# adaLN weights read by column halves, with a fixed order of loads, half sums over k for two units, and unread matmuls

## The chip, the core and the metric

The kernel is one program on one core of a Trainium2 chip. A core has a matrix engine (PE; the loads of its stationary operand are listed apart as PEld), a vector engine (DVE), a scalar engine (ACT), GpSimd (POOL), and SP, which here only issues DMAs. Each engine works through its own list of instructions in order and waits at semaphores for the others. The metric is the device time of one execution in microseconds (us), the median of several runs.

## The reference, cut to what matters

The layer is a diffusion-transformer block over 1024 latent tokens and 256 context tokens, width 1024. Only its beginning concerns this change: a conditioning vector gives a shift and a scale for each channel, the normalised tokens are scaled and shifted by them, and the result goes through one wide input projection.

```python
mod_lat = jax.nn.silu(c) @ w_ada[l] + b_ada[l]          # c: (1, 1024), w_ada: (1024, 6 * 1024)
mod_ctx = jax.nn.silu(c_ctx) @ w_ada[l] + b_ada[l]
sh1, sc1, gt1, sh2, sc2, gt2 = jnp.split(mod_lat[:, None, :], 6, axis=-1)
...
h_lat = modulate(rmsnorm(x_lat, norm_pre_mix[l]), sh1, sc1)   # h * (1 + scale) + shift
h_ctx = modulate(rmsnorm(x_ctx, norm_pre_mix[l]), csh1, csc1)
... = jnp.split(h_lat @ w_in, SPLITS, axis=-1)                # w_in: (1024, 4096)
```

Attention, a gated linear recurrence, the output projection and a 16-expert mixture follow; the change does not touch them.

## The kernel before, in words

Channel index d is cut into KT = 8 groups of 128, called k. The start stage does the following.

**The adaLN product** (lines 584 to 592). Of `w_ada` the first 2048 columns (shift, then scale) are needed here. A load (`load_ada`, line 500) brings one k and 1024 columns, 512 KB in pieces of 4 KB, into one of six buffers `aw`; sixteen loads bring all. Two matmuls per load add to one PSUM tile `mod_ps`, which the vector engine has cleared. After the sixteenth the tile is copied (lines 602, 603), transposed (607), and three DVE instructions make the columns `scc` and `shc` for all 8 values of k (618 to 620).

**The tokens.** They come as ten tiles of 128, in pairs p = 0 to 4 (pair 4 is the context). For each tile ACT squares and sums (`square_x`, 577), DVE and POOL make the reciprocal root (105, 106), DVE scales the tile (582). `trans_pair` transposes a pair on PE, 16 transposes into four PSUM tiles `tpx`, each for two values of k. `mod_pair` applies scale and shift: for k with k % 4 > 1 on ACT (646), else on DVE (648), then splits the result into a rounded high part on ACT (651) and the rest on DVE (652), four values of k in one instruction. The high and low parts `h_hi`, `h_lo` are what the projection reads.

**The projection.** A `Job` is a slice of columns of `w_in`; its weights are loaded (141) and split likewise into `whi` and `wlo` (150, 151). The first job has 256 columns, and `unit_N` makes one unit of it: two token tiles, 8 values of k, three matmuls for each (hi by hi, lo by hi, hi by lo: 185 to 187), 48 matmuls of 256 columns. Five units, one for each pair, make the first job; `ev_v` (258) copies a finished unit out, so this copy marks the end of a unit. The first unit is issued as two halves, one token tile each.

**What sets the order.** Within `manual_schedule` (line 521 to 670) PE, DVE and ACT run in the order of the code; SP is not in that set. Outside, a scheduler lays out each engine's list when the program is built. All loads spoken of are issued by SP: first the sixteen of `w_ada`, then the tokens' tiles 0 and 1, the first job's weights, the other tiles. The ring of `aw` buffers also holds the two context tiles.

Of the kernel before, what the change touches and what calls it, by code (L numbers as in the profile page):

```python
# [8 lines left out]
F32 = mybir.dt.float32  # L9
# [11 lines left out]
D = 1024  # L21
# [52 lines left out]
def layer(ctx: ExitStack, tc, a, out):  # L74
# [57 lines left out]
    class Job:  # L132
# [4 lines left out]
        def load(self):  # L137
            kk = 1024 // self.w
            for g in range(KT // kk):
# [4 lines left out]
        def split(self):  # L144
            kk = 512 // self.w
            for g in range(KT // kk):
# [25 lines left out]
    def unit_N(job, ppool, t, halves=False):  # L172

        pp = []

        def half(j):
            def f():
                if j == 0:
                    pp.append(ppool.tile([128, 512], F32, name="pp", bufs=2))
                o = pp[0][:, j * 256:(j + 1) * 256]  # L180
                c, z = divmod(t + j, 4)
                s = slice(z * 128, (z + 1) * 128)
                for k in range(KT):
                    whi, wlo = job.piece(job.hi, k), job.piece(job.lo, k)
                    nc.tensor.matmul(o, h_hi[c][:, k, s], whi, start=(k == 0), stop=False)  # L185
                    nc.tensor.matmul(o, h_lo[c][:, k, s], whi, start=False, stop=False)  # L186
                    nc.tensor.matmul(o, h_hi[c][:, k, s], wlo, start=False, stop=(k == KT - 1))
                if j == 1:
                    job.evac(pp[0], t)
            return f  # L190
        a, b = half(0), half(1)

        def both():
            a()
            b()
        return [a, b] if halves else both
# [297 lines left out]
    ps_p, ps_st = pool("start_ps", space=PSUM)  # L494
    mod_p, mod_st = pool("mod_ps", space=PSUM)
# [4 lines left out]
    def load_ada(i):  # L500
        aw = st_p.tile([128, 1024], F32, name="aw", bufs=6)
        nc.sync.dma_start(aw, adaw[:, i // 2, i % 2 * 1024:(i % 2 + 1) * 1024])
        aw_t.append(aw)

    def load_x(i):
# [7 lines left out]
        else:  # L513
            xts[i] = st_p.tile([128, D], F32, name="aw", bufs=6)
        nc.sync.dma_start(xts[i], a[src].rearrange("o (i p) d -> (o i) p d", p=128)[j])

    for k in range(6):
        load_ada(k)
# [8 lines left out]

    mod_ps = mod_p.tile([128, 512], F32, name="mod_ps")
    nc.vector.memset(mod_ps, 0.0)
# [20 lines left out]
    def small_vectors():  # L550
        nc.vector.tensor_copy(masks.rearrange("p l s -> p (l s)"), mf[:, :masks.shape[1] * 64])

        cols_ps = ps_p.tile([128, 512], F32, name="tp", bufs=2)
# [30 lines left out]
    for i in range(2 * KT):  # L584
        if i == 8:
            small_vectors()
        for n in range(2):
            q = 64 * (i % 2) + 32 * n
            nc.tensor.matmul(mod_ps[q:q + 2, :], silu[:, i // 2, :], aw_t[i][:, n * 512:(n + 1) * 512],
                             start=(i < 2), stop=(i // 2 == KT - 1))  # L590
        if i + 6 < 2 * KT:
            load_ada(i + 6)
    load_x(0)
    load_x(1)
    jobs[0].load()
    for i in range(2, 6):
        load_x(i)
    jobs[1].load()
    for i in range(6, 10):
        load_x(i)  # L600
    mods = st_p.tile([128, 512], F32, name="mods")
    nc.scalar.copy(mods[:, 0:256], mod_ps[:, 0:256])
    nc.vector.tensor_copy(mods[:, 256:512], mod_ps[:, 256:512])
    mod_st.close()
    modc_ps = ps_p.tile([128, 512], F32, name="tp", bufs=2)
    for j in range(4):
        nc.tensor.transpose(modc_ps[:, 128 * j:128 * j + 128], mods[:, j * 128:(j + 1) * 128], ident)
    shc = const.tile([128, KT, 2], F32, name="shc")
    scc = const.tile([128, KT, 2], F32, name="scc")

    mc = modc_ps.rearrange("p (j m n z) -> p m n j z", j=4, m=2, n=2)[:, :, :, :, 0:2]

    def four(ap):
        return ap.rearrange("p (n j) c -> p n j c", n=2)

    def both(i):
        return four(cols[:, i:i + 8, None].to_broadcast([128, 8, 2]))
    nc.vector.tensor_tensor(four(scc), mc[:, 1], both(34), op=OP.add)
    nc.vector.scalar_tensor_tensor(four(scc), four(scc), 1.0, both(0), op0=OP.add, op1=OP.mult)
    nc.vector.tensor_tensor(four(shc), mc[:, 0], both(26), op=OP.add)  # L620
    square_x(0)
    scale_x(0)
    square_x(1)
    scale_x(1)

    tp_p, tp_st = pool("tp_ps", space=PSUM)
    tps = {}

    def trans_pair(p):

        for g in range(4):
# [6 lines left out]
    def mod_pair(p):  # L638
# [3 lines left out]
        hf = [st_p.tile([128, 4, 256], F32, name="hf", bufs=2) for g in range(2)]  # L642
        for k in range(KT):
            tp, o = tps[p, k // 2][:, k % 2, :], hf[k // 4][:, k % 4, :]
            if k % 4 > 1:
                nc.scalar.activation(o, tp, AF.Identity, scale=scc[:, k, j:j + 1], bias=shc[:, k, j:j + 1])
            else:
# [1089 lines left out]
```

## Time and profile before

| | us |
|---|---|
| median of 3 runs | 1536.4 (1534.77 to 1536.62) |
| the profiled execution, own time | 1533.79 |
| its span in the profile | 1532.0 |
| first matmul of the first unit | 40.65 |
| copy of the fifth unit's result begins | 80.54 |

All times below are microseconds from the start of the span. In the timeline view each row has start, duration, engine, line, operation, output<-input, shape, count; in square brackets stands how long the engine had been idle and what released it. Consecutive equal instructions are merged in one row with their count. The line numbers of the kernel before and of the changed one differ: 185 to 187 become 189 to 191, 589 becomes 598, 636 becomes 628, 648 becomes 641, 652 becomes 645, 582 becomes 585, 502 becomes 506, 515 becomes 519.

### The profile page before, as it was taken

How to read it: one execution, taken by the hardware profiler on the slowest of the kernel's cores; microseconds unless marked ns; L12 is line 12 of the kernel's file. 1: busy time of each engine (PE TensorE's matmuls, PEld its weight loads, DVE VectorE, ACT ScalarE, POOL GpSimd, SP SyncE). 2: the span in 40 equal slices, each digit the busy share in tenths (PEclk: the TensorE clock that was granted, in tenths of full speed). 3: DMA queues.
4: the chain of work that ended last, by engine and by line, in shares of the span. 5: the costliest groups of instructions: out<-in, count | busy, mean ns of one | idle time of the engine just before them, and what ended most of it. 6: DMA issues, size and time to landing. Idle time of an engine off the chain costs nothing. (4 is left out here: it accounts for less than half of the span.)

```text
span 1532.0 us, 23371 instructions
## 1 busy us (share of the span) xinstructions
PE 1451.2 (95%) x8889; PEld 1193.5 (78%) x8889; DVE 1155.3 (75%) x1578; ACT 871.8 (57%) x1342; POOL 127.5 (8%) x139
## 2 busy tenths in 40 slices
PE   5999999999999997999999978999999999999993
PEld 1888998888977786999977845888888888888871
DVE  2727472859268668999936577999999999999984
ACT  2733442444211107988943324888888888888881
POOL 2100000000000001011001000111111111100013
PEclk9999999999999998999999999999999999999997
DMA  9210110100056617236026696999999999999966
GB/s 336 88 55 29 29 29 28 29 28 29 17 180 195 184 37 196 54 78 183 29 96 247 225 340 234 369 378 383 383 383 383 383 383 375 380 385 385 380 208 124
DMA packets 160332, 316.28 MB, mean 206 GB/s; under 512 B 13790, under 2 KB 50870, under 8 KB 160220
## 3 DMA queue, kind: packets, MB, share of 16 engines
q1 hardware_dynamic: 149616, 277.99, 50.4%
q0 software_dynamic: 9408, 33.54, 9.3%
q10 hardware_dynamic: 1196, 3.26, 0.6%
q8 instruction: 70, 1.15, 0.3%
q14 instruction: 42, 0.34, 0.1%
HBM read 274.36 MB, written 29.38 MB: 198 GB/s over the span
## 5 line engine op out<-in xcount | busy, mean ns | idle before, releaser
L1396 DVE TENSOR_TENSOR mlo<-mraw,mhi 128x1024 fp32r<-128x1024 f32 x332 | 398.2, 1223 | 19.1 <-ACT mhi L1395 15.0
L1395 ACT CAST mhi<-mraw 128x1024 fp32r<-128x1024 f32 x332 | 348.4, 1051 | 78.7 <-PE g L1546 28.8
L166 PE MATMUL pp<-h_hi,whi 128*128 128x512 f32 (+1 forms) x480 | 180.1, 375 | 0.0
L167 PE MATMUL pp<-h_lo,whi 128*128 128x512 f32 (+1 forms) x480 | 178.3, 371 | 0.0
L168 PE MATMUL pp<-h_hi,wlo 128*128 128x512 f32 (+1 forms) x480 | 178.0, 371 | 0.0
L150 ACT CAST whi<-wraw 128x512 fp32r<-128x512 f32 x64 | 39.6, 621 | 121.1 <-PE pp L167 59.1
L881 DVE TENSOR_REDUCE sm<-s 128x1 f32<-128x1280 f32 x64 | 95.3, 1491 | 13.1 <-PE s L876 10.7
L166 PEld LDWEIGHTS pp<-h_hi,whi 128*128 128x128 f32 x480 | 90.5, 188 | 17.6 <-ACT T L478 0.9
L168 PEld LDWEIGHTS pp<-h_hi,wlo 128*128 128x128 f32 x480 | 90.4, 188 | 17.1 <-issue 1.7
L1545 PE MATMUL g<-mhi,xhi 128*128 128x512 f32 x256 | 102.2, 399 | 0.5 <-ACT xhi L1525 0.5
L167 PEld LDWEIGHTS pp<-h_lo,whi 128*128 128x128 f32 x480 | 90.5, 189 | 15.6 <-issue 0.9
L1547 PE MATMUL g<-mlo,xhi 128*128 128x512 f32 x256 | 101.2, 395 | 0.2
L1546 PE MATMUL g<-mhi,xlo 128*128 128x512 f32 x256 | 101.1, 395 | 0.0
L1545 PE MATMUL u<-mhi,xhi 128*128 128x512 f32 x256 | 101.0, 394 | 0.0
L1547 PE MATMUL u<-mlo,xhi 128*128 128x512 f32 x256 | 100.9, 394 | 0.0
L1546 PE MATMUL u<-mhi,xlo 128*128 128x512 f32 x256 | 100.7, 393 | 0.0
L1650 PE MATMUL my<-mhi,hlo 128*128 128x512 f32 x240 | 97.7, 407 | 0.0
L1649 PE MATMUL my<-mhi,hhi 128*128 128x512 f32 x240 | 95.6, 398 | 0.0
L1651 PE MATMUL my<-mlo,hhi 128*128 128x512 f32 x240 | 95.2, 396 | 0.0
L185 PE MATMUL pp<-whi,h_hi 128*128 128x256 f32 x320 | 92.7, 290 | 2.0 <-ACT h_hi L651 2.0
L343 DVE TENSOR_TENSOR X<-X,T 128x640 f32<-128x640 f32 (+1 forms) x112 | 78.2, 761 | 20.4 <-ACT KM L321 12.8
L186 PE MATMUL pp<-whi,h_lo 128*128 128x256 f32 x320 | 91.8, 287 | 0.9 <-DVE h_lo L652 0.9
(331 smaller groups left out, 3149.5 us busy)
## 6 DMA issues: line engine op xcount, KB each, us to landing
mraw<-in_w_down_dram SPq DMA_DIRECT2D x128, 512.0 KB
mraw<-in_w_gate_dram SPq DMA_DIRECT2D x106, 512.0 KB
mraw<-in_w_up_dram SPq DMA_DIRECT2D x106, 512.0 KB
wraw<-in_w_in_dram SPq DMA_DIRECT2D x32, 512.0 KB
aw<-in_w_ada_dram SPq DMA_DIRECT2D x64, 256.0 KB
T<-in_w_gate_dram SPq DMA_DIRECT2D x22, 512.0 KB
T<-in_w_up_dram SPq DMA_DIRECT2D x22, 512.0 KB
aw<-in_w_ada_dram SPq DMA_DIRECT2D x16, 512.0 KB
```

What stands on the lines that cost most here:

```text
L166: nc.tensor.matmul(pp[:, :n], whi, hh, start=(k == 0), stop=False)
L167: nc.tensor.matmul(pp[:, :n], whi, hl, start=False, stop=False)
L168: nc.tensor.matmul(pp[:, :n], wlo, hh, start=False, stop=(k == KT - 1))
L881: nc.vector.tensor_reduce(self.sm[:, m:m + 1], s, axis=AX.X, op=OP.max, negate=True)
L1395: nc.scalar.copy(hi, r)
L1396: nc.vector.tensor_sub(lo, r, hi)
L1545: nc.tensor.matmul(o, x.hi[:, k, :], hi[:, kk, :], start=(k == 0), stop=False)
L1546: nc.tensor.matmul(o, x.lo[:, k, :], hi[:, kk, :], start=False, stop=False)
L1547: nc.tensor.matmul(o, x.hi[:, k, :], lo[:, kk, :], start=False, stop=(k == 7))
L1649: nc.tensor.matmul(y[:, ns], x.hh[:, k, :], hi[:, ns], start=(k == 0), stop=False)
L1650: nc.tensor.matmul(y[:, ns], x.hl[:, k, :], hi[:, ns], start=False, stop=False)
L1651: nc.tensor.matmul(y[:, ns], x.hh[:, k, :], lo[:, ns], start=False, stop=(k == 7))
```

## The change

1. `w_ada` is read by column halves: a load now brings one k and 2 x 512 columns (half of the shift columns and the same half of the scale columns, pieces of 2 KB). Eight loads make the first half (k groups 0 to 3 of `scc`, `shc`), eight more the second. Each half has its own clear, copy, transposes and three DVE instructions (`ada_out`). The ring has seven buffers, and the PSUM tile `tp` has one buffer in place of two.
2. SP joins the manual order: tokens 0 and 1, the eight loads of the first half, the first job's weights around tokens 2 and 3, the eight of the second half, then the rest.
3. `unit_N` takes `parts`: for the first two units part 0 sums k = 0 to 3 for both token tiles, part 1 the rest. A matmul of zeros opens the PSUM tile. `trans_pair` and `mod_pair` can do one half of the values of k.
4. `keep_on` issues matmuls whose result nobody reads: ten after the first `ada_out`, eight after the second.

The diff, cut:

```diff
-    def unit_N(job, ppool, t, halves=False):
+    def unit_N(job, ppool, t, parts=1):
...
+                    if parts > 1:
+                        nc.tensor.matmul(pp[0], zero1[:, 0:128], zero1, start=True, stop=False)
+                for j in range(2):
...
+                    for k in range(i * KT // parts, (i + 1) * KT // parts):
...
     def load_ada(i):
-        aw = st_p.tile([128, 1024], F32, name="aw", bufs=6)
-        nc.sync.dma_start(aw, adaw[:, i // 2, i % 2 * 1024:(i % 2 + 1) * 1024])
+
+        aw = st_p.tile([128, 2, 512], F32, name="aw", bufs=7)
+        src = adaw[:, i % KT, 0:2 * D].rearrange("p (m c) -> p m c", m=2)
+        nc.sync.dma_start(aw, src[:, :, i // KT * 512:(i // KT + 1) * 512])
...
-    ms = tc.manual_schedule(engines={nc.tensor.engine, nc.vector.engine, nc.scalar.engine})
+    ms = tc.manual_schedule(engines={nc.tensor.engine, nc.vector.engine, nc.scalar.engine, nc.sync.engine})
     ms.__enter__()
+    load_x(0)
+    load_x(1)
+    for k in range(KT - 1):
+        load_ada(k)
...
+    def ada_mm(i):
+
+        if i % KT == 0:
+            mod_ps.append(mod_p.tile([128, 512], F32, name="mod_ps"))
+            nc.vector.memset(mod_ps[-1], 0.0)
+        for m in range(2):
+            nc.tensor.matmul(mod_ps[-1][32 * m:32 * m + 2, :], silu[:, i % KT, :], aw_t[i][:, m, :],
+                             start=(i % KT == 0), stop=(i % KT == KT - 1))
...
+    u0, u1 = (unit_N(jobs[0], pps, t, parts=2) for t in (0, 2))
+    norm_pair(0)
+    for i in range(KT):
+        ada_mm(i)
+        if i == 0:
+            load_ada(KT - 1)
+            jobs[0].load(0)
+            load_x(2)
+            load_x(3)
+            jobs[0].load(1)
+        else:
+            load_ada(KT - 1 + i)
+        if i == 3:
+            small_vectors()
+            trans_pair(0)
+    load_ada(2 * KT - 1)
+    load_x(4)
+    load_x(5)
+    jobs[1].load()
+    for i in range(6, 10):
+        load_x(i)
+    ada_out(0)
+    jobs[0].split(0)
+    mod_pair(0, (0,))
+    keep_on(10)
+    u0[0]()
     norm_pair(1)
-    u0[0]()
-    trans_pair(1)
+    jobs[0].split(1)
+    ada_mm(8)
+    trans_pair(1, (0, 1))
+    ada_mm(9)
+    ada_mm(10)
+    mod_pair(1, (0,))
+    ada_mm(11)
+    ada_mm(12)
+    u1[0]()
+    for i in range(13, 16):
+        ada_mm(i)
+    ada_out(1)
+    keep_on(8)
+    mod_pair(0, (1,))
+    trans_pair(1, (2, 3))
+    mod_pair(1, (1,))
+    norm_pair(2)
     u0[1]()
+    trans_pair(2, (0, 1))
+    u1[1]()
+    trans_pair(2, (2, 3))
     ms.__exit__(None, None, None)
```

From the sixth unit on the lists of all engines hold the same rows in the same order as before. Three places where they differ follow.

SP's loads at the start, before (-) and now (+); `outT_hg` and `xpair` are the tokens' tiles, `aw` the adaLN weights, `wraw` the projection's:

```order
-L502 DMA aw<-in_w_ada_dram 128x1024 x16
-L515 DMA outT_hg_77<-in_x_dram 128x1024 x2
-L141 DMA wraw<-in_w_in_dram 128x4x256 x2
-L515 DMA outT_hg_78<-in_x_dram 128x1024 x2
-L515 DMA xpair<-in_x_dram 128x1024 x2
+L519 DMA outT_hg_77<-in_x_dram 128x1024 x2
+L506 DMA aw<-in_w_ada_dram 128x2x512 x8
+L141 DMA wraw<-in_w_in_dram 128x4x256
+L519 DMA outT_hg_78<-in_x_dram 128x1024 x2
+L141 DMA wraw<-in_w_in_dram 128x4x256
+L506 DMA aw<-in_w_ada_dram 128x2x512 x8
+L519 DMA xpair<-in_x_dram 128x1024 x2
```

The tokens 0 and 1 stand ahead of all weights now, and tokens 2 and 3 and the first job's weights ahead of the second half of `w_ada`.

The vector engine from the first shift and scale on, first before (`outT_hg_77` are tokens 0 and 1, `outT_hg_78` tokens 2 and 3):

```order
L620 TENSOR_TENSOR shc<-tp,cols 128x16
L105 TENSOR_SCALAR st<-st 128x1
L582 TENSOR_SCALAR outT_hg_77<-outT_hg_77,st 128x1024
L105 TENSOR_SCALAR st<-st 128x1
L582 TENSOR_SCALAR outT_hg_77<-outT_hg_77,st 128x1024
L151 TENSOR_TENSOR wlo<-wraw,whi 128x512 x4
L648 TENSOR_SCALAR hf<-tpx,scc,shc 128x256 x4
L652 TENSOR_TENSOR h_lo_85<-hf,h_hi_84 128x4x256 x2
```

and now:

```order
L617 TENSOR_TENSOR shc<-tp,cols 128x8
L151 TENSOR_TENSOR wlo<-wraw,whi 128x512 x2
L641 TENSOR_SCALAR hf<-tpx,scc,shc 128x256 x2
L645 TENSOR_TENSOR h_lo_85<-hf,h_hi_84 128x4x256
L105 TENSOR_SCALAR st<-st 128x1
L585 TENSOR_SCALAR outT_hg_78<-outT_hg_78,st 128x1024
L105 TENSOR_SCALAR st<-st 128x1
L585 TENSOR_SCALAR outT_hg_78<-outT_hg_78,st 128x1024
L151 TENSOR_TENSOR wlo<-wraw,whi 128x512 x2
L596 MEMSET mod_ps 128x512
L641 TENSOR_SCALAR hf<-tpx,scc,shc 128x256 x2
L645 TENSOR_TENSOR h_lo_85<-hf,h_hi_84 128x4x256
```

The clear of the second half's `mod_ps` stands behind the scaling of tokens 2 and 3 and the split of the second piece of weights; the ninth adaLN product on PE needs it.

PE around the transposes of tokens 4 and 5, which the changed program issues between part 1 of the first unit (`pp_299`) and part 1 of the second (`pp_374`):

```order
L190 MATMUL pp_299<-whi_341,h_lo0_85 128x256
L191 MATMUL pp_299<-wlo_342,h_hi0_84 128x256
L628 MATMUL tpx_490<-ident_67,xpair_250 128x128 x4
L628 MATMUL tpx_495<-ident_67,xpair_250 128x128 x4
L189 MATMUL pp_374<-whi_337,h_hi0_84 128x256
L190 MATMUL pp_374<-whi_337,h_lo0_85 128x256
```

Before, the transposes of tokens 4 and 5 (`xpair_225`) stood behind the whole first unit (`pp_328`) and ahead of the whole second one (`pp_494`):

```order
L186 MATMUL pp_328<-whi_298,h_lo0_85 128x256
L187 MATMUL pp_328<-wlo_299,h_hi0_84 128x256
L636 MATMUL tpx_428<-ident_67,xpair_225 128x128 x4
L636 MATMUL tpx_433<-ident_67,xpair_225 128x128 x4
L636 MATMUL tpx_438<-ident_67,xpair_225 128x128 x4
L636 MATMUL tpx_443<-ident_67,xpair_225 128x128 x4
L185 MATMUL pp_494<-whi_286,h_hi0_84 128x256
L186 MATMUL pp_494<-whi_286,h_lo0_85 128x256
```

In both programs the unit behind the transposes cannot begin until tokens 4 and 5 are scaled.

## Rows read from the trace of the kernel before

**Rows 1.** The page: span, busy time of each engine, GB/s in 40 equal slices.
```profile
span 1532.0 us, 23371 instructions
PE 1451.2 (95%) x8889; PEld 1193.5 (78%) x8889; DVE 1155.3 (75%) x1578; ACT 871.8 (57%) x1342; POOL 127.5 (8%) x139
GB/s 336 88 55 29 29 29 28 29 28 29 17 180 195 184 37 196 54 78 183 29 96 247 225 340 234 369 378 383 383 383 383 383 383 375 380 385 385 380 208 124
```

**Rows 2.** Windows: PE, PEld, DVE, ACT, POOL busy us; granted clock; DMA share; GB/s.
```profile
25.00:30.00 5.00, 3.99 (x18) 0.37 (x16) 0.00 (x0) 0.00 (x0) 0.00 (x0) 1.00 1.02 407
35.00:40.00 5.00, 3.33 (x15) 3.06 (x15) 4.44 (x9) 3.39 (x7) 0.00 (x0) 0.67 1.05 382
40.00:45.00 5.00, 3.47 (x15) 3.28 (x16) 3.24 (x5) 4.89 (x9) 0.94 (x2) 0.68 1.06 396
45.00:50.00 5.00, 5.00 (x45) 5.00 (x44) 3.80 (x9) 4.31 (x9) 1.26 (x3) 0.98 0.53 157
70.00:75.00 5.00, 5.00 (x44) 5.00 (x43) 0.62 (x1) 0.22 (x1) 0.00 (x0) 1.00 0.02 3
```

**Rows 3.** Timeline, 0 to 82 us: adaLN products, shift and scale, units one and five.
```profile
16.52 0.09 PEld L589 LDWEIGHTS mod_ps<-aw,silu 128*2 128x2 f32 x4 [1.21 <-DMA aw<-in_w_ada_dram]
21.64 0.09 PEld L589 LDWEIGHTS mod_ps<-aw,silu 128*2 128x2 f32 x4 [1.19 <-DMA aw<-in_w_ada_dram]
29.32 1.03 PE L589 MATMUL mod_ps<-aw,silu 128*2 128x512 f32 x4 [0.26 <-DMA aw<-in_w_ada_dram]
32.06 0.17 DVE L620 TENSOR_TENSOR shc<-tp,cols 128x16 f32<-128x16 f32 x1
40.65 0.38 PE L185 MATMUL pp<-whi,h_hi 128*128 128x256 f32 x1 [2.04 <-ACT h_hi L651]
74.78 0.65 ACT L258 COPY V<-pp 128x256 f32<-128x256 f32 x2 [5.06 <-PE pp L187]
80.54 0.65 ACT L258 COPY V<-pp 128x256 f32<-128x256 f32 x2 [0.22 <-PE pp L187]
```

**Rows 4.** Lines by form, 0 to 82 us: count, busy us, mean ns.
```profile
L652 DVE TENSOR_TENSOR h_lo<-hf,h_hi 128x1024 fp32r<-128x1024 f32 x10 | 11.8, 1221 | 1.7 <-ACT h_hi L651 1.7
L651 ACT CAST h_hi<-hf 128x1024 fp32r<-128x1024 f32 x10 | 10.1, 1059 | 0.4 <-DVE hf L648 0.4
L648 DVE TENSOR_SCALAR hf<-tpx,scc,shc 128x256 f32<-128x256 f32 x20 | 10.0, 538 | 0.0
L646 ACT ACTIVATE hf<-tpx,shc,scc 128x256 f32<-128x256 f32 x20 | 10.3, 568 | 2.8 <-PE tpx L636 2.3 <-DVE h_lo L652 0.4
L151 DVE TENSOR_TENSOR wlo<-wraw,whi 128x512 fp32r<-128x512 f32 x8 | 5.2, 687 | 8.3 <-ACT whi L150 8.3
```

**Rows 5.** Timeline: squares of tokens 2 and 3, scaling of token 3.
```profile
41.44 1.06 ACT L577 ACTIVATE sq<-outT_hg 128x1024 bf16<-128x1024 f32 x1
45.20 0.75 DVE L582 TENSOR_SCALAR outT_hg<-outT_hg,st 128x1024 f32<-128x1024 f32 x1 [0.66 <-POOL st L106]
```

**Rows 6.** Timeline, PE: 256-column matmuls at the low clock, transposes at either.
```profile
43.14 0.41 PE L185 MATMUL pp<-whi,h_hi 128*128 128x256 f32 x1
43.35 0.41 PE L186 MATMUL pp<-whi,h_lo 128*128 128x256 f32 x1
35.28 3.33 PE L636 MATMUL tpx<-ident,outT_hg 128*128 128x128 f32 x15 [1.10 <-DVE outT_hg L582]
50.80 1.91 PE L636 MATMUL tpx<-ident,xpair 128*128 128x128 f32 x16
```

**Rows 7.** Timeline: SP's issue on an idle queue, ACT's wait for that landing.
```profile
79.63 1.81 SPq L141 DMA_DIRECT2D wraw<-in_w_in_dram  x2
84.00 0.62 ACT L150 CAST whi<-wraw 128x512 fp32r<-128x512 f32 x1 [2.81 <-DMA wraw<-in_w_in_dram]
```

**Rows 8.** Lines by form, whole span: matmuls whose result nobody reads.
```profile
L1360 PE MATMUL s<-onesb 128*128 128x512 bf16 x75 | 18.6, 379 | 0.0
```

**Rows 9.** Timeline, PE: a transpose with other matmuls queued behind it.
```profile
55.41 0.30 PE L636 MATMUL tpx<-ident,xpair 128*128 128x128 f32 x1 [0.67 <-DVE xpair L582]
```

More of the change, by code (lines that the diff above doesn't have):

```diff
@@ L135, in __init__, with load @@
             self.raw, self.hi, self.lo = [], [], []
-        def load(self):
+        def load(self, part=None):
             kk = 1024 // self.w
-            for g in range(KT // kk):
+            for g in range(KT // kk) if part is None else (part,):
                 r = wp.tile([128, kk, self.w], F32, name="wraw", bufs=2)
@@ L142, in load, with split @@
                 self.raw.append(r)
-        def split(self):
+        def split(self, part=None):
             kk = 512 // self.w
-            for g in range(KT // kk):
+            for g in range(KT // kk) if part is None else (2 * part, 2 * part + 1):
                 r = self.raw[g // 2][:, (g % 2) * kk:(g % 2 + 1) * kk, :]
@@ L170, in unit_T, with part @@
         return f
-    def unit_N(job, ppool, t, halves=False):
+    def unit_N(job, ppool, t, parts=1):
         pp = []
-        def half(j):
+        def part(i):
             def f():
-                if j == 0:
+                if i == 0:
                     pp.append(ppool.tile([128, 512], F32, name="pp", bufs=2))
[L180 to L188, printed above, removed]
+                    if parts > 1:
+                        nc.tensor.matmul(pp[0], zero1[:, 0:128], zero1, start=True, stop=False)
+                for j in range(2):
+                    o = pp[0][:, j * 256:(j + 1) * 256]
+                    c, z = divmod(t + j, 4)
+                    s = slice(z * 128, (z + 1) * 128)
+                    for k in range(i * KT // parts, (i + 1) * KT // parts):
+                        whi, wlo = job.piece(job.hi, k), job.piece(job.lo, k)
+                        nc.tensor.matmul(o, h_hi[c][:, k, s], whi, start=(k == 0 and parts == 1), stop=False)
+                        nc.tensor.matmul(o, h_lo[c][:, k, s], whi, start=False, stop=False)
+                        nc.tensor.matmul(o, h_hi[c][:, k, s], wlo, start=False,
+                                         stop=(k == KT - 1 and (j == 1 or parts == 1)))
+                if i == parts - 1:
                     job.evac(pp[0], t)
             return f
[L191 to L196, printed above, removed]
+        fs = [part(i) for i in range(parts)]
+        return fs if parts > 1 else fs[0]
     jobs = []
@@ L582, in scale_x @@
         nc.vector.tensor_scalar(xts[i], xts[i], st[:, 1:2], None, op0=OP.mult)
[L584 to L607, printed above, removed]
     shc = const.tile([128, KT, 2], F32, name="shc")
@@ L621, in layer, with ada_out, both @@
[L621 to L626, printed above, removed]
+    mod_ps = []
+    def ada_mm(i):
[5 more added lines that the diff above has]
+                             start=(i % KT == 0), stop=(i % KT == KT - 1))
+    def ada_out(hf):
+        mods = st_p.tile([128, 512], F32, name="mods")
+        nc.scalar.copy(mods[:, 0:256], mod_ps[hf][:, 0:256])
+        nc.vector.tensor_copy(mods[:, 256:512], mod_ps[hf][:, 256:512])
+        modc = ps_p.tile([128, 512], F32, name="tp")
+        for j in range(4):
+            nc.tensor.transpose(modc[:, 128 * j:128 * j + 128], mods[:, j * 128:(j + 1) * 128], ident)
+        mc = modc.rearrange("p (j r) -> p j r", j=4)
+        def both(i):
+            i += 4 * hf
+            return cols[:, i:i + 4, None].to_broadcast([128, 4, 2])
+        sc, sh = scc[:, 4 * hf:4 * hf + 4, :], shc[:, 4 * hf:4 * hf + 4, :]
+        nc.vector.tensor_tensor(sc, mc[:, :, 32:34], both(34), op=OP.add)
+        nc.vector.scalar_tensor_tensor(sc, sc, 1.0, both(0), op0=OP.add, op1=OP.mult)
+        nc.vector.tensor_tensor(sh, mc[:, :, 0:2], both(26), op=OP.add)
@@ L627, in layer, with trans_pair @@
     tps = {}
-    def trans_pair(p):
-        for g in range(4):
+    def trans_pair(p, gs=range(4)):
+        for g in gs:
             tp = tps[p, g] = tp_p.tile([128, 2, 256], F32, name="tpx", bufs=4)
```

54 lines of the change are left out of this document (25 added, 29 removed).

## The prediction

> **What bounds the kernel now.** I read the page first, then the windows of the start stage, then the timeline there. The page shows a matmul engine that is busy 95% of a span of 1532.0 us [rows 1]; all the change edits lies in the first 81. In the windows PE works 3.3 to 3.5 of 5 us until 45, at a mean clock of 0.67 and 0.68, and 5 of 5 afterwards; from 70 on DVE and ACT have next to nothing to do (0.62 and 0.22 us of 5) while PE is full [rows 2]. The timeline gives the chain: the sixteenth adaLN load is multiplied at 29.32, shift and scale are known at 32.06 + 0.17 = 32.23, the first unit starts at 40.65, the fifth is copied out at 80.54 [rows 3]. So 80.5 is the end of the stage. Behind it the lists of all engines are the same rows in the same order, and DVE, ACT and the loads of the next job have slack there in both programs; whatever the end of the fifth unit moves by, the end of the kernel moves by. The question is when PE finishes unit five.
>
> **The rates.** A unit of 48 matmuls takes 80.54 - 74.78 = 5.76 us at full clock, 0.12 each [rows 3]; at the low clock starts are 0.21 apart [rows 6]. Sixteen transposes take 1.91 at full clock and fifteen 3.33 at the low one [rows 6]; without the tail of the last (0.3) that is 0.10 and 0.20 each. For DVE and ACT: `h_lo` 1.22, `h_hi` 1.06, a pair of `hf` 1.0, a `wlo` 0.65 when they follow each other [rows 4]. A norm pair, from the start of its first square on ACT to the end of its second scaling on DVE, takes 45.20 + 0.75 - 41.44 = 4.5 us [rows 5].
>
> **The head start.** Tokens 0 and 1 and eight loads now come ahead: ten 512 KB loads, where before sixteen loads lay before the shift. Before, the tenth load released PE at 21.64 [rows 3]. The pieces are 2 KB, not 4: before, 4 KB pieces ran at 407 GB/s [rows 2] and the expert stage, with loads of 2 KB and of 4 KB pieces, at 383 [rows 1], so eight loads (4.2 MB) cost 0 to 0.7 us more; I take 0.4, and it does not decide, since PE is later. The sixth load is there at 16.52 [rows 3]; PE then ends two products at about the low clock (to 18.7, at twice 0.9), does the column transposes (0.3) and 16 transposes (1.6 to 3.3), and four products of 0.9 to 1.03 each: 24.2 to 26.4, of which I take 24.5. From the last product to the shift took 32.23 - 30.35 = 1.9 us, so the first half is known at 26.4. Two `wlo` (1.3), two `hf` (0.9) and one `h_hi` (1.06) later PE starts unit one at 29.6, 11 us earlier than before. That part is a real gain. What remains is whether it lasts.
>
> **Where it is given back.** Part 0 of unit one is 24 matmuls, 2.9 to 5.1 us, done by 35. The ninth product needs the second clear of `mod_ps`. That stands on DVE behind `h_lo`, a norm pair and two `wlo`: squares start at 29.5, the pair is scaled at 34.1, the splits end at 35.3, the clear (0.4) at 35.7. Only then does product 8 run, to 36.7, and only its end frees the buffer of the sixteenth load. On an idle queue a load took 84.00 - 79.63 = 4.4 us from issue [rows 7], so it lands at 41.2; the queue behind it (tokens 4 to 9, the next job) waits too, and all of it is still early. PE goes on: 8 transposes to 37.3, then the second pair's `hf`, `h_hi`, `h_lo` (1.4 + 1.06 + 1.22 with gaps) to 41.1, beside which products 9 to 12 run (3.7 us, to 41.1). Part 0 of unit two takes 2.9, to 44.1; the last three products 2.8, to 46.9; 1.8 more and the second half of shift and scale is known at 48.7. Before, all of it was known at 32.2: for k = 4 to 7 that is 16 us later.
>
> From 48.7: `hf`, `h_hi`, `h_lo` of pair 0 end at 52.0. The eight unread matmuls cost 18.6 / 75 = 0.25 each [rows 8], 2.0 in all, and with 8 transposes PE is at 51.5, hidden below the 52.0. Part 1 of unit one ends at 55.0. Then PE's list has transposes of tokens 4 and 5. Their squares stand on ACT behind the second half of pair 1, whose `h_hi` ends at 54.0; 4.5 us on they are scaled, at 58.6. PE stands idle from 55.0 to 58.6, with part 1 of unit two, ready since 55, queued behind. The trace of before has the pattern: at 55.41 a transpose waited 0.67 us for the scaled tokens, with matmuls of the second unit behind it [rows 9].
>
> [...]
>
> After 3.6 us without work I expect the low clock: the windows of 35 to 40 and 40 to 45, in which PE waits and works by turns, have means of 0.67 and 0.68 [rows 2]. So 8 transposes to 60.1, and part 1 of unit two in 4.0 (between 2.9 and 5.1) to 64.1; 8 more transposes to 64.9. Now DVE is what is late: `hf` pair, `h_lo`, an `hf`, the root and scaling of the last context tile between, another `hf`, then `h_lo` of pair 2's second half; together 2 x 0.45 + 1.15 + 2 x 0.45 + 1.1 + 1.22 = 5.3, to 70.2. Unit three can do 13 of its 48 matmuls before that. Left at 70.2: 35 + 96 = 131 matmuls of 0.12 and 8 transposes, 15.7 + 0.8, so unit five ends at 86.7 against 80.5. **Loss 6.2 us.** Against the profiled execution, 1533.79 + 6.2 = 1540.0; the median of the runs lies 2.6 above that execution, and I predict the same of the change: 1536.4 + 6.2 = 1542.6.
>
> **Parts that cost nothing by themselves.** The two matmuls of zeros (0.25 each by [rows 8]) and the ten unread matmuls (2.5 to 3.4) end before `h_hi` at 29.5; if that cover goes, they cost up to 1 us. Extra small instructions (a second clear, copies, three DVE operations) are counted above. The seventh buffer and SP's order keep the loads ahead of PE until the sixteenth, which PE takes at 46, 5 us after it landed.
>
> **The clock.** It is the largest unknown. With the full clock all through, the first half is known 1 us sooner, and the stretch from 58.6 to 64.9 takes 4.6 instead of 6.3, of which DVE gives back part: end 84.7, loss 4.2. With the low clock in more of 40 to 60 (part 0 of unit two, the last products and the unread matmuls at twice their time, 2.5 us net), 89.2, loss 8.7. [...]
>
> **Rivals.** (A) Faster: the head start lasts. It would if the second half followed its loads: 12 loads after 21.64 at 1.28 each ((29.32 - 21.64) / 6) are in at 37, shift and scale at 40, part 1 of unit one at 43.4. PE then has 192 matmuls and 56 transposes left, 23 + 5.8, and DVE and ACT need some 6 us for each further pair: end 74.5, 1530.4. For it speaks the early 29.6. Against it speaks the place of the clear, behind a norm pair on DVE, and the two queue places above. It decides for this side if product 8 runs before 33 and tokens 4 and 5 are scaled before 55. (B) No measurable change: the full clock, and a wait for tokens 4 and 5 of about 2 us (squares that get in between ACT's other work faster than in [rows 5]); end 82 to 83.5, 1539. For it: PE's low clock before 45 goes away. Against it: DVE's order before unit three. (C) Slower still, by the low clock as above: 1545.1. (D) The change does not do what it says, a load or unit in the same place as before: the lists exclude it.
>
> **How the numbers follow.** About 0.2%, 3.1 us, is what a measurement of this kernel tells from no change. Forecast 0.61, C 0.20, B 0.12, A 0.07. So slower 0.81, same 0.12, faster 0.07. The likeliest case is 1542.6, with 4.2 to 8.7 of loss its own range (1540.6 to 1545.1). To hold 8 of 10 I add the spread of the runs (1.8) above and reach into B below: 1538.0 to 1546.5.
>
> **What would show it.** Unit one starting near 29.6 and the ten loads in by 22 confirm the head start. The clear near 35.7, product 8 behind it, and `shc` of the second half near 48.7 confirm the first half of the loss; PE idle some 3 us before the transposes of tokens 4 and 5, and `h_lo` of pair 2's second half near 70, the second. Were the fifth copy at or before 80.5, or the time after it to the end changed by over 1 us, the prediction is wrong.

## The result, and the profile after

The changed kernel takes 1548.76 us (median of six runs) where the kernel before takes 1536.82 in the same session: ratio 1.0069, 95% interval 1.0055 to 1.0082. A second series of the same program gave 1.0076 (1.0062 to 1.0090). (The ratio is an estimate with its interval; it is not the quotient of the two medians, which is 1.0078.) It is slower, as forecast, but by some 10 to 12 us instead of 6.2; 1542.6 was forecast, and 1548.76 lies above the range.

The page after, against [rows 1]: the span, and the busy time of each engine.

```profile
span 1547.4 us, 23414 instructions
PE 1463.8 (95%) x8913; PEld 1201.8 (78%) x8913; DVE 1157.9 (75%) x1585; ACT 873.4 (56%) x1343; POOL 128.4 (8%) x139
```

The span grew by 15.4 us, 12.6 of them in PE's busy time, though PE has only 24 matmuls more. Those 24 are the 18 unread ones, two of zeros and four more transposes of the adaLN sums, some 6 us at 0.25 [rows 8]. Most of the rest we put down to the lower clock, an estimate: up to PE's last matmul the trace's clock records hold 44 us at 0.50 after and 31 before. The profiled execution took 1549.18, close to its median; that of before took 1533.79, 3 us under its own. So the two profiles overstate the loss.

The start stage follows the prediction step by step. PE and DVE in the timeline, against [rows 3]:

```profile
26.16 0.16 DVE L617 TENSOR_TENSOR shc<-tp,cols 128x8 f32<-128x8 f32 x1
29.61 0.38 PE L189 MATMUL pp<-whi,h_hi 128*128 128x256 f32 x1 [0.59 <-ACT h_hi L644]
35.09 0.48 DVE L596 MEMSET mod_ps<- 128x512 f32 x1
35.63 1.03 PE L598 MATMUL mod_ps<-aw,silu 128*2 128x512 f32 x4 [0.24 <-DVE mod_ps L596]
48.96 0.16 DVE L617 TENSOR_TENSOR shc<-tp,cols 128x8 f32<-128x8 f32 x1
51.31 1.23 DVE L645 TENSOR_TENSOR h_lo<-hf,h_hi 128x1024 fp32r<-128x1024 f32 x1 [1.17 <-ACT h_hi L644]
57.44 0.33 PE L628 MATMUL tpx<-ident,xpair 128*128 128x128 f32 x1 [1.83 <-DVE st L105]
58.98 1.75 PE L628 MATMUL tpx<-ident,xpair 128*128 128x128 f32 x7 [1.21 <-DVE xpair L585]
65.62 0.65 ACT L259 COPY V<-pp 128x256 f32<-128x256 f32 x2 [1.85 <-PE pp L191]
88.43 0.65 ACT L259 COPY V<-pp 128x256 f32<-128x256 f32 x2 [0.22 <-PE pp L191]
```

The first half of shift and scale is known at 26.3, unit one starts 11 us earlier than before. Then the second half is known at 49.1, 17 us later than all of it was; PE stands 1.83 + 1.21 us for tokens 4 and 5 (the 1.83 carries the label of a small DVE step; behind it stands the scaling that ends at 57.4), and the fifth unit is copied out at 88.43 instead of 80.54.

The windows, against [rows 2] (PE, PEld, DVE, ACT, POOL busy; granted clock; DMA share; GB/s):

```profile
35.00:40.00 5.00, 4.75 (x28) 1.68 (x28) 1.64 (x4) 2.06 (x3) 0.00 (x0) 1.00 0.67 217
55.00:60.00 5.00, 1.96 (x12) 1.57 (x11) 2.54 (x6) 4.51 (x10) 1.10 (x2) 0.83 0.00 0
60.00:65.00 5.00, 5.00 (x25) 5.00 (x24) 3.27 (x8) 2.99 (x5) 1.65 (x3) 0.50 0.02 5
70.00:75.00 5.00, 4.44 (x37) 4.18 (x37) 4.85 (x7) 4.54 (x7) 0.00 (x0) 1.00 0.00 0
```

Between 35 and 40 products keep PE fuller, with its clock at 1.00 where [rows 2] have 0.67. At 55 to 60 PE works 2 of 5 us, and in the window behind it the clock is 0.50, the lower of the two values that the clock records of both traces hold (0.50 and 1.00): 25 matmuls in five full microseconds. At 70 to 75 DVE and ACT are full, where before they had 0.62 and 0.22 us to do.

So the start stage is 7.9 us longer. Two more profiles of the changed kernel, below, have the copy at 87.31 and 87.94, and a second one of before at 80.76: 7.2 in the mean. That is the 6.2 of the sum, within its range of 4.2 to 8.7. But 7.5 us more are lost behind the fifth copy, where the prediction had nothing: the time from there to the end is 1451.5 in the profile of before and 1459.0 in that of after. Row by row, the delay of after's PE against before's stays at 7.9 until the first row product of the later adaLN. DVE and PE there, before:

```profile
448.43 0.75 DVE L742 SCALAR_TENSOR_TENSOR acc<-aw,silu,acc 128x512 f32<-128x512 f32 x1 [0.40 <-DMA aw<-in_w_ada_dram]
450.50 1.02 PE L748 MATMUL mp<-acc,onesc 128*1 128x512 f32 x2 [1.56 <-DVE acc L742]
```

and after:

```profile
458.52 0.75 DVE L787 SCALAR_TENSOR_TENSOR acc<-aw,silu,acc 128x512 f32<-128x512 f32 x1 [2.38 <-DMA aw<-in_w_ada_dram]
460.59 1.44 PE L793 MATMUL mp<-acc,onesc 128*1 128x512 f32 x2 [3.86 <-DVE acc L787]
```

DVE works here on eight loads `aw` for one row, and the row product on PE needs all eight. The seventh of them comes 2 us later, and PE waits 2.3 us longer, though nothing was edited within 360 us of it.

### The profile page after: what moved, and what is told of

It reads as the page before. It is cut to its first block, busy times and chain, and to the rows that moved or that the text cites. A ratio compares the mean times of both kernels' runs of the same rounds, so it can differ in the third digit from the quotient of the medians.

```text
span 1547.4 us, 23414 instructions
## 1 busy us (share of the span) xinstructions
PE 1463.8 (95%) x8913; PEld 1201.8 (78%) x8913; DVE 1157.9 (75%) x1585; ACT 873.4 (56%) x1343; POOL 128.4 (8%) x139
```

## Experiments on the part behind the fifth unit

Three theories. **Shift**: a start stage that ends later costs more behind it, whatever the reason of the delay. **Program pieces**: a DMA queue of its own (70 packets of 16 KB, below) carries what we take for PE's program, and the 45 instructions that PE has more at the start move these pieces to other places. **Spread**: executions of one program differ there. The expectations call them S, P and E, and add a theory M, that buffers lie at other addresses. The 45 are 48 matmuls and weight loads more and three semaphore instructions fewer.

The page's DMA table has that queue (queue, kind: packets, MB, share):

```profile
q8 instruction: 70, 1.15, 0.3%
```

70 packets of 16 KB for 2 x 8913 matmuls and weight loads: one for some 255 of them, so we take them for PE's program. The DMA view of the 6 us in which the load is under way, after (452 to 458):

```profile
q1 hardware_dynamic: 1085, 1.54, 83.1%
q8 instruction: 1, 0.02, 2.0%
```

and before (443 to 449):

```profile
q1 hardware_dynamic: 1008, 1.41, 74.7%
```

After, one piece falls into the load, at 453.42; before, none does: it comes at 452.98, 2.48 us behind the row product, too late to matter.

**before_pad23.** Shifts the pieces alone: 46 instructions in the kernel before.

```diff
+    for _ in range(23):
+        nc.tensor.matmul(pad_ps[0:1, 0:64], warm0[:, 0:1], warm0, start=True, stop=True)
```

> The kernel before with 23 small unread matmuls (1 column of weights, 64 columns) ahead of the first adaLN product, while PE has nothing else to do; every other row of every engine is as before. PE's list is 46 instructions longer, as that of the changed kernel is 45 longer. Three theories for the 7.5 us that the changed kernel lost after the fifth copy. Theory P (place of PE's code loads): PE's code comes in pieces of 16 KB by DMA (70 of them in the trace), one piece every 128 matmuls, and with 45 instructions more one of them falls beside a load that DVE and PE wait for at 450 us. Then the fifth copy stays at 80.5 (+-0.5), PE's wait before the first row product of the later adaLN part grows from 1.56 us to 3 or more, and the total is 3 to 7 us above before. Theory S (shift in time): the start alone was late, and whatever runs by its own time (the granted clock) met the rest in a worse phase. Then nothing changes here: total within 1.5 us of before. Theory M (buffers at other addresses): also within 1.5 us.

Ratio 1.0012 (1.0004 to 1.0021), fifth copy at 80.56 as before. At the row product:

```profile
449.60 0.75 DVE L747 SCALAR_TENSOR_TENSOR acc<-aw,silu,acc 128x512 f32<-128x512 f32 x1 [1.60 <-DMA aw<-in_w_ada_dram]
451.67 1.12 PE L753 MATMUL mp<-acc,onesc 128*1 128x512 f32 x2 [2.69 <-DVE acc L747]
```

The piece now comes at 446.78, while the load is under way, and the wait is there in the old kernel: 1.60 instead of 0.40, 2.69 instead of 1.56. All of it costs 1.6 us by the medians and 1.8 by the ratio, less than the 3 to 7 expected. The run also adds a small buffer with its clear and a PSUM tile; after_pad50 below has the same and no such wait, so it is the count of instructions that decides, and not the buffer.

**after_pad105** and **after_pad50** do the reverse in the changed kernel, with 105 and 50 such matmuls: the piece comes 2.4 us behind the row product, or 14 ahead of it.

> The changed kernel with 105 such small unread matmuls ahead of the first adaLN product: PE's list is then 45 + 210 = 255 instructions longer than before, one code piece of 256, so that from the sixth unit on the code loads fall where they fell before. Theory P: the wait before the first row product goes back to below 2 us (3.86 in the changed kernel), and the time after the fifth copy is 3 to 5 us shorter than in the changed kernel; the fifth copy itself at 88.4 or up to 1 us earlier (the unread matmuls may raise the clock at the start). Ratio to before 1.003 to 1.005. Theories S and M: the later loss stays at 7.5 us, ratio 1.007.

> The changed kernel with 50 small unread matmuls (1 column of weights, 64 columns) ahead of the first adaLN product: PE's list is 145 instructions longer than before, so that the code piece lands about 11 us further ahead of the first row product than in the changed kernel (7.2 us ahead there), clear of the load that it met. Theory P: wait before the first row product below 2 us, ratio 0.001 to 0.002 below that of the changed kernel run beside it. If the place of the code does not matter: wait as in that kernel, 2.5 us or more, same ratio.

1546.07, ratio 1.0051 (1.0037 to 1.0065), and 1546.76, 1.0067 (1.0053 to 1.0080). In both the wait is gone; here after_pad50:

```profile
455.74 0.75 DVE L792 SCALAR_TENSOR_TENSOR acc<-aw,silu,acc 128x512 f32<-128x512 f32 x1 [0.33 <-DMA aw<-in_w_ada_dram]
457.81 1.02 PE L798 MATMUL mp<-acc,onesc 128*1 128x512 f32 x2 [1.88 <-DVE acc L792]
```

Against after's 1.0069 the ratios fall by 2.8 and 0.3 us (after_pad50 by 1.4 against the 1.0076 of after_again, which ran beside it); the intervals overlap, so what the wait costs in the runs can't be read from these two. The profiles still need 1457.4 and 1457.1 us behind the fifth copy. The wait belongs to the pieces; it is not the 7.5.

**before_late8.** Shifts everything: sixteen small dependent DVE steps ahead of the first shift and scale.

```diff
+    for _ in range(16):
+        nc.vector.tensor_scalar(mods, mods, 1.0, None, op0=OP.mult)
```

> The kernel before with 16 multiplications by one of 128x512 on DVE (0.47 us each) between the copy of the adaLN sums and their transposes: shift and scale known some 7.6 us later, PE's list unchanged in number. Theory S: the fifth copy comes 6 to 8 us later, and the time after it grows by 4 to 7 us more, as in the changed kernel: ratio 1.007 to 1.009. Theory P: the fifth copy 6 to 8 us later and the time after it unchanged within 1.5 us: ratio 1.004 to 1.005. Theory M: as P.

Fifth copy at 90.40, 9.9 later; 1548.21, ratio 1.0068 (1.0054 to 1.0081), that is 10.4 us. The row product waits as in the kernel before (0.14 on DVE, 1.60 on PE), and the loss is the delay and hardly more (the interval leaves 8.3 to 12.5). Its profile needs 1456.6 us behind the fifth copy, 5.1 more than the first of before, which taken alone would speak for the shift; before_again shows below that the same kernel differs by more. Here a shift of 9.9 us alone cost 10.4.

**after_again**, **after_third** and **before_again** are the same two programs once more.

> The changed kernel once more, without an edit. The later loss was read from one profiled execution of each kernel (7.5 us), and that of before lies 3.9 us below the median of its 20 runs so far (1537.7). Theory P (code loads): the wait before the first row product is again above 2.5 us, as PE's list is the same, and the median is 10 to 12 us above before, 2 to 4 of these after the fifth copy. If the later loss was only the luck of one execution, that wait is below 2 us now and the ratio 1.005 (the 7.9 us of the start stage alone).

> The changed kernel, unchanged, a third profile. Theory P: 1457 to 1460 us after the fifth copy, as in the first profile, and the second (1454.3) was the odd one. Theory E: anywhere from 1454 to 1460 us. If the piece of TensorE's program that comes in beside the load of the later adaLN's weights belongs to the kernel: DVE waits over 1.5 us for that load and TensorE over 2.5 us before the first row product; if its place were chance, under 1 us and under 2 us. Fifth copy 87.2 to 88.5.

> The kernel before, unchanged, against itself: ratio 1.000 to within 0.001, and a second profile of it. Theory P (the time after the fifth V copy belongs to the program, and the kernel before simply needs 1451.5 us there): a second profile gives 1450.5 to 1452.5 us after the fifth copy. Theory E (it differs by a few us from one execution to the next, and the profiled execution of before, 3 us under its own median, had a short one): 1453 to 1457 us. Both: fifth copy at 80.5 +- 0.3, wait of TensorE before the first row product of the later adaLN 1.4 to 1.8 us.

The kernel before against itself: 1.0007 (0.9994 to 1.0019). Its second profile has the fifth copy at 80.76, the wait of 1.69 at the row product, and 1459.1 us behind the fifth copy: 7.6 more than in its first profile, and as much as after's first. The changed kernel's second and third needed 1454.3 and 1456.0, each with the long wait (2.96 and 2.80). So the wait belongs to the program, in three profiles of three, and most of the 7.5 to the execution: the first profile of before is the shortest there of all 18. What differs from one to the next is mostly the clock. Windows 440:520, 560:640 and 880:960 of the first profile of before:

```profile
440.00:520.00 80.00, 76.49 (x457) 64.30 (x456) 61.95 (x104) 9.85 (x18) 0.00 (x0) 1.00 0.59 182
560.00:640.00 80.00, 69.11 (x419) 60.55 (x418) 66.36 (x80) 54.84 (x99) 7.19 (x14) 0.91 0.44 107
880.00:960.00 80.00, 63.50 (x421) 40.07 (x420) 63.18 (x143) 28.38 (x43) 4.33 (x5) 0.96 0.81 286
```

and of the second:

```profile
440.00:520.00 80.00, 74.79 (x431) 62.78 (x430) 60.20 (x101) 7.86 (x14) 0.00 (x0) 0.98 0.61 183
560.00:640.00 80.00, 69.88 (x396) 60.45 (x395) 62.81 (x76) 50.44 (x90) 6.19 (x12) 0.89 0.41 100
880.00:960.00 80.00, 63.30 (x411) 39.87 (x410) 58.27 (x141) 24.72 (x40) 4.89 (x6) 0.91 0.78 275
```

The shortfall of the clock, times 80, is 10.4 us in the first and 17.6 in the second: 7.2 more, an upper bound of what the clock takes of the 7.6, as not all work there waits for PE. After's first profile has 0.98, 0.89 and 0.91 in the same windows 8 us later, its second 1.00, 0.89 and 0.96. Over all 18 profiles of this study the time behind the fifth copy (1451 to 1459) is 0.42 times the length of the low clock there (20 to 41 us, up to PE's last matmul) plus 1.28 times PE's idle time (37 to 42), plus a constant, to within 0.6 us each: a fit, by which 5.7 of the 7.6 are clock and 1.6 idle time. So a profile pair shows nothing there under some 8 us until the low stretches are taken out.

## Experiments on the start stage

**after_units_first.** Tests the queue step: part 1 of unit two goes ahead of the transposes that wait for tokens 4 and 5.

```diff
-    trans_pair(2, (0, 1))
     u1[1]()
-    trans_pair(2, (2, 3))
+    trans_pair(2)
```

> The changed kernel with all 16 transposes of tokens 4 and 5 behind part 1 of unit two instead of half of them ahead of it (the scheduler orders a few rows of units three to five anew). If the queue on PE cost what the prediction says (part 1 of unit two ready at 55 to 56, blocked until 58.9, then at the low clock): copy of unit two at 59.5 to 61 instead of 65.6, PE's wait for tokens 4 and 5 about 0.5 to 1 us in place of 3.0, fifth copy 2 to 4 us earlier (84.5 to 86.5). Rival: DVE's order before unit three holds everything anyway (h_lo of pair 2's second half at 71): unit two early, fifth copy within 1 us of 88.4.

1542.62, ratio 1.0031 (1.0018 to 1.0045). V copies two and five:

```profile
59.72 0.63 ACT L259 COPY V<-pp 128x256 f32<-128x256 f32 x2
84.51 0.65 ACT L259 COPY V<-pp 128x256 f32<-128x256 f32 x2 [0.22 <-PE pp L191]
```

Unit two ends 5.9 us earlier, unit five 3.9: the matmuls that stood ready behind a waiting transpose were worth about half of the stage's loss.

**after_fill_wait.** The order stays; thirteen unread matmuls stand in the wait.

```diff
     u0[1]()
+    keep_on(13)
     trans_pair(2, (0, 1))
```

> The changed kernel with 13 more unread matmuls (0.235 us each, 3.1 us) between part 1 of unit one and the transposes of tokens 4 and 5, where PE stood idle (1.83 and 1.21 us). If idleness there lowered the clock (58.3 to 65.1 us in the changed kernel) and the low clock cost 2.5 to 3 us, part 1 of unit two runs at 0.12 a matmul, the copy of unit two comes at 62.5 to 63.5 and the fifth 1 to 2.5 us earlier. If the low clock there had another cause, the copy of unit two stays at 65.6 or later. For the later part (theory P): PE's list is 26 instructions longer than the changed kernel's, 71 longer than before, so the code piece lands some 3 us further ahead of the row product at 450 and misses the awaited load: wait there below 2 us.

1544.27, ratio 1.0051 (1.0035 to 1.0067). PE in the wait, and the two copies:

```profile
55.13 2.98 PE L662 MATMUL tp<-warm 128*128 128x512 bf16 x13
58.68 0.98 PE L628 MATMUL tpx<-ident,xpair 128*128 128x128 f32 x7 [0.46 <-DVE st L105]
62.59 0.65 ACT L259 COPY V<-pp 128x256 f32<-128x256 f32 x2
85.82 0.65 ACT L259 COPY V<-pp 128x256 f32<-128x256 f32 x2 [0.22 <-PE pp L191]
```

The wait is as long as it was, but seven transposes behind it take 0.98 instead of 1.75, unit two ends 3.0 earlier and unit five 2.6 (2.1 against the mean of after's three profiles). We read that as the clock's share of the wait; in after the clock records hold 0.50 there, from 58.3 to 65.1.

**after_no_unread.** Both `keep_on` calls taken out.

> The changed kernel without its 18 unread matmuls (ten and eight); nothing else moves. PE's list is then 9 instructions longer than before. Theory P: the code load misses the awaited load, the later loss falls from 7.5 us to below 4. Theories S and M: it stays at 7.5. For the start stage: by the prediction the unread matmuls end before the values that PE waits for, so without them unit one starts at 29.6 at the same place, and the fifth copy is at 88.4 if the clock is as before, up to 2 us later if they held it up (part 0 of unit one and part 1 at the low clock).

1544.79, ratio 1.0048 (1.0032 to 1.0064), so not slower than after; but its fifth copy is at 89.40, and unit one's first products wait and run slow:

```profile
31.43 0.58 PE L189 MATMUL pp<-whi,h_hi 128*128 128x256 f32 x1 [3.46 <-ACT h_hi L644]
30.00:35.00 5.00, 2.89 (x12) 2.60 (x13) 2.50 (x6) 4.28 (x7) 1.10 (x2) 0.63 1.05 387
```

(the second row is the window 30 to 35). The 1 to 1.5 us that the stage loses are small beside the spread behind it, so this run settles little on the unread matmuls. early_kept below does. For the program pieces it settles more: PE's list is only 9 instructions longer than before's, the piece comes 1.5 us behind the row product, and the long wait is gone (0.25 on DVE, 1.82 on PE).

**after_clear.** Tests the step "the ninth product needs the second clear": the clear goes right behind the first half's shift (and the first clear ahead of the products).

```diff
     ada_out(0)
+    ada_clear()
     jobs[0].split(0)
```

> The changed kernel with the second clear of mod_ps moved up on DVE, right behind the first shift and scale (26.3 us) and ahead of the splits, the first h_lo and the norm pair; nothing else moves. My prediction put the start of the second half's late products on this clear (35.1 to 35.6 us in the changed kernel). If it decides, product 8 starts some 5 us earlier and the second half of shift and scale is known at 44 to 46 instead of 49.1, the fifth copy 2 to 4 us earlier. Rival: on PE product 8 also stands behind part 0 of unit one, whose last matmul is issued near 35.3, so the clear waits for nobody in particular: product 8 starts at 35.2 to 35.6, second half at 48.5 to 49.1, fifth copy 88.4 +-1.

1546.05, ratio 1.0061 (1.0044 to 1.0077), fifth copy at 88.61. DVE and PE:

```profile
27.37 0.48 DVE L594 MEMSET mod_ps<- 128x512 f32 x1
36.83 1.03 PE L599 MATMUL mod_ps<-aw,silu 128*2 128x512 f32 x4
```

The clear is there 7.7 us earlier, and product 8 starts no earlier, 9.6 us behind the first half's shift, where the changed kernel has 9.3. What holds it is its place on PE, behind part 0 of unit one: from 32.4 on PE goes without a gap from matmul to matmul of that part, most of them 0.21 us apart at the low clock, until product 8 follows. The window 32.4 to 36.8:

```profile
32.40:36.80 4.40, 4.40 (x23) 4.29 (x23) 2.77 (x5) 1.94 (x4) 1.10 (x2) 0.61 0.91 336
```

The clear was no cause.

**products_early.** So the products of the second half are moved on PE: 8 ahead of part 0 of unit one, 9 to 11 right behind it, all ahead of unit two, whose part 1 goes ahead of the transposes. The clears are early and the unread matmuls out.

```diff
     mod_pair(0, (0,))
-    keep_on(10)
+    ada_mm(8)
     u0[0]()
...
-    ada_mm(8)
+    for i in range(9, 12):
+        ada_mm(i)
     trans_pair(1, (0, 1))
-    ada_mm(9)
-    ada_mm(10)
     mod_pair(1, (0,))
-    ada_mm(11)
-    ada_mm(12)
-    u1[0]()
-    for i in range(13, 16):
+    for i in range(12, 16):
         ada_mm(i)
     ada_out(1)
-    keep_on(8)
+    u1[0]()
...
-    trans_pair(2, (0, 1))
     u1[1]()
-    trans_pair(2, (2, 3))
+    trans_pair(2)
```

> The changed kernel with the second clear early, no unread matmuls, product 8 ahead of part 0 of unit one, products 9 to 15 right behind it and ahead of part 0 of unit two, and the transposes of tokens 4 and 5 behind part 1 of unit two. Theory: the loss of the start stage is the place of the second half's products on PE (their loads are there by 38), not the halving as such. Then the second half is known at 42 to 44 instead of 49.1, the fifth copy comes at 79 to 81 (88.4 in the changed kernel, 80.5 before), and the ratio is 0.998 to 1.002. Rival (halving itself, with twice the chains of shift and scale and half-size instructions, costs the time): fifth copy at 84 or later, ratio 1.002 to 1.005. Theory P: PE's list is 8 to 9 instructions longer than before, so the wait at 450 is below 2 us.

1538.82, ratio 1.0014 (1.0003 to 1.0026): most of the loss is gone. The second half is known at 46.1 (49.1), the fifth copy is at 81.84. But PE waits for the ninth load, and its clock falls:

```profile
29.85 1.87 PE L599 MATMUL mod_ps<-aw,silu 128*2 128x512 f32 x4 [3.04 <-DMA aw<-in_w_ada_dram]
30.00:35.00 5.00, 5.00 (x18) 2.92 (x15) 2.54 (x5) 4.28 (x7) 1.10 (x2) 0.50 1.05 387
```

**early_kept.** Eight unread matmuls into that wait.

```diff
+    keep_on(8)
     ada_mm(8)
```

> products_early with one edit: eight unread matmuls (1.9 us) between the first shift and scale and product 8, where PE had waited 3.04 us for the ninth load and the clock then fell (29.3 to 36.1 us, all of part 0 of unit one at 0.21 a matmul). If the idleness lowered the clock, part 0 of unit one is mostly at 0.12 now and the second half of shift and scale is known 1.5 to 3 us earlier (46.1 before), the fifth copy at 79 to 80.5 (81.84 before): ratio to before 0.998 to 1.001. If not, as products_early: fifth copy 81 to 82.5.

1537.20, ratio 0.9997 (0.9988 to 1.0006). The same two rows:

```profile
29.87 1.03 PE L599 MATMUL mod_ps<-aw,silu 128*2 128x512 f32 x4 [0.72 <-DVE hf L642]
30.00:35.00 5.00, 4.22 (x28) 2.97 (x25) 2.65 (x5) 4.24 (x7) 1.10 (x2) 1.00 1.05 388
```

Product 8 starts at the same time, but takes 1.03 instead of 1.87, the second half is known at 44.4, and the fifth copy is at 80.18. The clock is 1.00 in every window of 5 us from 25 to 45 and from 50 to 75. Here unread matmuls are worth 1.7 us.

**reordered_kept**, **early_squares**, **early_squares2** look for a gain from there: the norm work of each later pair on DVE and ACT is pulled ahead between `hf` and `h_lo` (reordered_kept: all later pairs; the other two: tokens 4 and 5 alone). The core of early_squares against early_kept, beside `square_x(4)` right behind `ada_out(1)` and the transposes of tokens 4 and 5 between the two parts 1:

```diff
-    mod_pair(0, (1,))
+    mod_hf(0, (1,))
+    square_x(5)
+    scale_x(4)
+    mod_lo(0, (1,))
```

In early_squares2, `square_x(5)` and `scale_x(4)` stand behind `mod_lo(0, (1,))`.

> early_kept with the rest of the start stage written out by hand as well: squares of tokens 4 and 5 on ACT ahead of the second half of pair 0, of 6 to 9 ahead of the h_hi that would block them, transposes of a pair right behind its scaling. By a count of the rows' durations in order this ends 1 to 2 us before early_kept: fifth copy at 77.5 to 80, ratio 0.996 to 1.000. Rival: DVE and ACT need some 7 us per pair whatever their order, and the fifth copy stays at 80 or later.

> Early_kept (products of the first adaLN's first columns ahead of unit one, unread matmuls ahead of product 8) with the squares and scaled copies of tokens 4 and 5 put ahead among DVE's and ACT's work on pair 0, and their transposes between part 1 of unit one and of unit two. Theory 1 (the wait of TensorE for the scaled tokens 4 and 5 is what is left in the start stage that earlier work can take away): fifth V copy at 77.5 to 79.5 instead of 80.2, ratio to before 0.997 to 0.9995. Theory 2 (DVE and ACT bound the stage from the first h on, so that any order of their work ends alike): fifth copy at 80 to 81.5, ratio 0.9995 to 1.001.

> As early_squares, but square and scaled copy of tokens 5 and 4 stand behind the low parts of pair 0's second half, not ahead of them. Theory 1: fifth V copy at 77.5 to 79.5, and unit two's part 1 starts earlier than in early_squares, since the low parts come earlier; ratio 0.997 to 0.9995. Theory 2: 80 to 81.5, ratio 0.9995 to 1.001.

1539.25, ratio 1.0014 (1.0005 to 1.0023); 1535.88, 0.9993 (0.9980 to 1.0006); 1536.92, 1.0000 (0.9987 to 1.0012). Fifth copies at 79.92, 79.42 and 80.96. The window 55 to 60 of early_squares:

```profile
55.00:60.00 5.00, 4.33 (x38) 4.14 (x37) 4.27 (x8) 4.41 (x9) 0.55 (x1) 1.00 0.01 3
```

All three engines are nearly full, so we read it that whichever work is pulled ahead, another `h_lo` is late; no run tests that alone. No version beats the kernel before by more than can be measured. Whether DVE and ACT could be relieved of work was not tried.

## Why the prediction was wrong

**Right, by its own steps.** First half of shift and scale (26.4; 26.3), unit one (29.6; 29.6), clear (35.7; 35.6), second half known (48.7; 49.1), `h_lo` of pair 0 (52.0; 52.5), tokens 4 and 5 scaled (58.6; 58.9), PE idle before their transposes (3.6; 1.83 + 1.21 around one transpose), low clock behind it (shown by after_fill_wait), matmuls queued behind it (shown by after_units_first). The stage was forecast 6.2 longer and is 7.2.

**Right value, wrong cause.** The clear at 35.7 was computed rightly and called what product 8 waits for. It did: 0.24 us. Two things end within a quarter of a microsecond there, and after_clear shows that the other, product 8's place on PE behind part 0 of unit one, holds it alone.

**The step that failed** is "whatever the end of the fifth unit moves by, the end of the kernel moves by". It took for granted that equal lists take equal time. The lists fixed the order, but not how long a load took: 45 instructions more put a piece into the load of the seventh `aw`, DVE waited 2.38 us for it instead of 0.40, and the wait at the first row product is 2.8 to 3.9 in three profiles of after, 1.6 and 1.7 in two of before, in the mean 1.6 us more. before_pad23 makes that wait in the old kernel, after_pad50 and after_pad105 take it from the new one. The prediction had named the sign itself: a time behind the fifth copy that changes by over 1 us. The rest of the 7.5 between the two profiles is no step of the kernel: before_again differs from before by 7.6 in the same part.

**How the loss adds up, and what is open.** The medians lie some 11.5 us apart, the means of all runs (twelve of after, 39 of before) 10.3. 7.2 are the start stage. The wait costs more than its 1.6 us: the second row product on PE, in the two profiles of before and the three of after,

```profile
464.30 1.02 PE L748 MATMUL mp<-acc,onesc 128*1 128x512 f32 x2
465.04 1.02 PE L748 MATMUL mp<-acc,onesc 128*1 128x512 f32 x2 [0.42 <-DVE acc L742]
476.19 1.02 PE L793 MATMUL mp<-acc,onesc 128*1 128x512 f32 x2 [0.33 <-DVE acc L787]
472.85 1.02 PE L793 MATMUL mp<-acc,onesc 128*1 128x512 f32 x2 [0.35 <-DVE acc L787]
474.47 1.02 PE L793 MATMUL mp<-acc,onesc 128*1 128x512 f32 x2
```

comes 383.8 and 384.3 us behind the fifth copy before, and 387.8, 385.5 and 386.5 after: 2.6 more in the mean. In the first and third profile of after the clock falls behind the wait (0.94 in the window 440 to 470 of both, 1.00 in that of the second), and the first row product takes 1.44 and 1.86 instead of 1.02. The mean times from the fifth copy to the end (1455.3 and 1456.5) differ by less, 1.2, but the three profiled executions of after held some 54 us of low clock, and its twelve runs some 58 by their mean granted clock of 0.981; the kernel before has 58 in its profiles and in its runs. At 0.42 for each us that is 1.7 more, an estimate: 7.2 + 1.2 + 1.7 = 10.1 of the 10.3. So the stage and the wait with what follows it make 9.8, and between 0.5 us (by the means) and 1.7 (by the medians) are in no row.

Of the rivals, C (slower still by the clock) named the right side, but its mechanism is not what happened: between 35 and 50 the clock was 1.00, and the loss beyond the forecast came mostly from behind the stage. A failed because the second half of the products is behind unit one on PE; with that undone (products_early, early_kept) the stage ends as before, not at 74.5, as DVE and ACT are nearly full in what follows (4.41 and 5.00 of 5 us in the window 60 to 65 of early_kept). One sum is slightly off: the range was to end 1.8 above 1545.1, which is 1546.9 and not 1546.5; neither reaches 1548.76.

## What to carry to other kernels

Unit one began 11 us earlier here and the stage still ended 7.2 later, as the other half of the sum stood behind it on PE. Look for what is queued behind each new wait and move the ready work ahead of it (unit two ended 5.9 us earlier in after_units_first), and try unread matmuls in a wait that can't go (fifth copy 1.7 and 2.6 us earlier here, in single profiles). Before two profiles are subtracted, take the same kernel's profile twice: behind the changed part this program differs by 7.6 us with itself. And where a wait appears in code that was not touched, count the instructions ahead of it before looking for a cause in the data: 46 more made such a wait in before_pad23 (2.69 us instead of 1.56).

## What was not expected of the hardware

A load came late where a piece of what we take for PE's program, 16 KB on its own DMA queue, fell into it: in six profiles (three of after, one each of after_units_first, after_clear and before_pad23), where the piece comes while the load of the seventh `aw` is under way on another queue, DVE waits 1.6 to 2.4 us for that load, and up to 0.5 us in ten others where it comes at another time. In after_fill_wait, where it ends 0.5 us ahead of the load's issue, the wait is 0.92. One kernel (reordered_kept) waits 1.14 without a piece, so something else can delay it too. The trace of after (70 packets, some 255 of PE's matmuls and weight loads for each) lists no wait of PE for a piece; the cost turns up on DVE, the reader of the other queue's load (2.38 us).
